# Splitting the low half of each dense weight block into four column pieces on GpSimd

## The chip, the cores and the metric

The kernel runs on one core of a Trainium2 chip. The metric is the time of one execution on the device in microseconds (us); lower is better. Three runs of the kernel before took 2069.74, 2070.41 and 2076.77 us, with a median of 2070.41 us.

The engines are named as in the profile: PE is the matrix engine (PEld its weight loads), DVE is VectorE, ACT is ScalarE, POOL is GpSimd, SP issues most of the transfers.

## The reference

One decoder block over 1024 tokens of width 1024, in float32, with 16 learned tokens put in front. A normalised input goes through two branches side by side, a short gated convolution and a stick-breaking attention with 16 heads of 64; sigmoid gates merge them, an output projection and a gated feed-forward network (width 2816) with a causal depthwise convolution follow.

```python
h = xn @ w_in                                   # (1040, 1024) @ (1024, 8192)
b_c, c_c, h_c, q, k, v, g_conv, g_attn = split(h)
branch_conv = (b_c * causal_dwconv(c_c * h_c, conv_w_mix)) @ w_proj_conv
branch_attn = stick_breaking_attention(q, k, v) @ w_proj_attn
merged = sigmoid(g_conv + b0) * branch_conv + sigmoid(g_attn + b1) * branch_attn
h = h + rms_norm(merged @ w_out)
u, g = split(rms_norm(h) @ w_up_gate)
h = h + rms_norm((gelu(causal_dwconv(u, conv_w_ffn)) * g) @ w_down)
# attention: A[t,s] = sigmoid(z_ts) * prod_{s<j<t} (1 - sigmoid(z_tj)), s < t
```

## The kernel before

**Split operands.** Every product of two float32 matrices is made of three matrix products of a narrower type. An operand x is split into a high half (a copy rounded to the narrower type, written by ACT) and a low half (x minus the high half). The helper `split` at L63 does both: L64 is the copy on ACT, L65 the subtraction on DVE or on the engine it is given. A product is then high·high (L124), high·low (L125) and low·high (L126).

**Dense items.** The class `Dense` (L80) runs a list of 80 items: 64 column blocks of `w_in` (values, queries, keys, the three parts of the convolution, and the two gates), then 8 of `w_proj_conv` and 8 of `w_proj_attn`. One item holds a weight block of 128 rows by 1024 columns: eight blocks of 128 columns, one for each part kb of the contraction. `load` (L96) starts the transfer of the block into a tile `raw`, `prep` (L103) makes the tiles `whi` and `wlo` from it, `run` (L112) prepares item i and i+1, loads i+2, and then issues the products of item i: three chunks of the tokens by eight kb by three products, and after each chunk an evacuation. `raw`, `whi` and `wlo` have two buffers each; a `raw` buffer comes free when the subtraction has read it. Products with the low half read only the 128 columns of `wlo` that belong to their kb.

**The attention beside it.** While the 64 items of `w_in` run, the attention of pair p of heads runs beside the items of pair p+1. `stage1` (L311) makes scores on PE (L326, L327), two sigmoids on ACT (L328 into `fl`, L329 into `be`), a running product over `fl` on DVE (the scan, L336), its product with `be` on POOL (L339), and a mask on POOL (L340). `stage2` (L353) transposes `be` on PE (L373), splits the result into `ah` (ACT) and `al` (DVE, L65), and multiplies it with the values on PE (L363, L364). The convolution of an item runs as `conv3` (L196): one pass on ACT (L197) and two on DVE (L198, L199) over the tile `yy`. The order of emission is a credit scheme written by hand, which spreads items evenly over the pairs; the framework that places instructions and waits can then move an instruction ahead of others on its engine.

**The start and the end of the dense items.** At the start, nine blocks of tokens are normalised (`x_block`, L449: the factor by small DVE operations L72 to L77, the scaling on DVE at L459 for the first three blocks, on POOL at L461 and DVE at L462 for the others) and transposed on PE (L179), with the first two weight blocks prepared between. At the end, each of the last eight items (`item_pa`, L605) multiplies a loaded gate with its result on DVE (L615) and adds on POOL (L616), while the blocks of `w_out` are loaded (L640) and split into the tiles `w_o`, the low half on POOL. These loads share the two `raw` buffers with the dense items, and SP issues them in order.

Of the kernel before, what the change touches and what calls it, by code (L numbers as in the profile page):

```python
# [8 lines left out]
F32 = mybir.dt.float32  # L9
F32R = mybir.dt.float32r  # L10
AF = mybir.ActivationFunctionType
ALU = mybir.AluOpType
# [3 lines left out]
D = 1024  # L16
# [16 lines left out]
def block_kernel(ctx, tc, x, meta_tokens, g_pre_mix, w_in, channels, w_proj_conv,  # L33
                 w_proj_attn, w_out, g_post_mix, g_pre_ffn, w_up_gate, w_down,
                 g_post_ffn, out):
    nc = tc.nc
# [26 lines left out]
    def split(hi, lo, src, lo_engine=None):  # L63
        nc.scalar.copy(hi, src)  # L64
        (lo_engine or nc.vector).tensor_tensor(lo, src, hi.bitcast(F32), op=ALU.subtract)  # L65
# [14 lines left out]
    class Dense:  # L80
# [22 lines left out]
        def prep(self, i):  # L103
            if i < len(self.items) and i not in self.hl:
                self.load(i)
                raw = self.raw.pop(i)
                hi = wpool.tile([P, D], F32R, name="whi", tag="whi")
                lo = wpool.tile([P, D], F32R, name="wlo", tag="wlo")
                split(hi, lo, raw, nc.gpsimd)
                self.hl[i] = (hi, lo)  # L110

        def run(self, i):  # L112
# [915 lines left out]
    for k, _ in enumerate(products(0, *HALF[1], bank_of(ps_o, "po"), evac_u(*HALF[1]))):  # L1028
        if k % 2:
            next(prep, None)  # L1030
# [40 lines left out]
    for i in range(1, len(pairs)):  # L1071
        p, gate = divmod(i, 2)
        if gate:
            conv_gelu(p)
            sets = [products(i, 1, 512, bank, evac_g(p))]
        else:
            sets = [products(i, j0, n, bank, evac_u(j0, n)) for j0, n in HALF]
        for _ in prep:
            pass
        prep = prep_pair(i + 1) if i < last_pair else prep_down_first()  # L1080
        for si, st in enumerate(sets):
            for k, _ in enumerate(st):
                if gate or (7 * si + k) % 2:
                    next(prep, None)
# [45 lines left out]
    for gi, fbs in enumerate(groups):  # L1130
# [14 lines left out]
        for tb in range(8):  # L1145
# [3 lines left out]
            for hf in range(2):  # L1149
                ps = bank()  # L1150
                c = slice(hf * 512, (hf + 1) * 512)
# [6 lines left out]
                a = accs[tb][:, c]  # L1158
# [4 lines left out]
                if last:  # L1163
                    sq = dw.tile([P, 512], F32, name="sq", tag="sq", bufs=2)
                    nc.scalar.activation(sq, a, AF.Square, accum_out=ssqs[tb][:, hf:hf + 1])
                    eng = nc.vector if (tb == 7 and hf) else nc.gpsimd
                    eng.tensor_tensor(a, a, g_post2[:, c], op=ALU.mult)
            next(prep, None)
            if last:
                a, hb, s0 = accs[tb], hbs[tb], ssqs[tb]  # L1170
                nc.vector.tensor_tensor(s0[:, 0:1], s0[:, 0:1], s0[:, 1:2], op=ALU.add)
                r = rstd_of(fsml, s0[:, 0:1], P)
                for hf in range(2):
                    c = slice(hf * 512, (hf + 1) * 512)
# [60 lines left out]
```

## Time and profile before

| | |
|---|---|
| median of 3 runs | 2070.41 us (2069.74 to 2076.77) |
| the profiled execution | 2079.27 us, of it the span from the first to the last instruction 2077.1 us |
| granted PE clock, mean | 0.991 |
| PE busy | 1988.1 us, 12228 matrix instructions |
| DVE busy | 1033.7 us |
| ACT busy | 851.9 us |
| POOL busy | 914.8 us |
| subtractions of the dense blocks on POOL | 80, of 2394 ns each in the mean, 191.5 us in all |

Reading it: "busy" is the time in which an engine has an instruction under way, also one that is held up after it has begun. In a group's row the columns are line, engine, operation, output and inputs, shapes, count; then busy time in us and the mean of one in ns; then the idle time of the engine just before the group's instructions and what ended it. In a row of the timeline the first number is the start in us from the beginning of the span, the second the duration; what stands in square brackets is the idle time before it and what ended that.

The kernel passes through the normalisation of the tokens (to about 60 us), the attention with the dense items of `w_in` (to about 987 us), the last gates and the two branch projections (to about 1262 us), the output projection (to about 1415 us), the up and gate products (to about 1826 us) and the down product.

### The profile page before, as it was taken

To read this page: it belongs to the slowest core of one execution; us is meant where nothing else is said; L and a number is where in the kernel's file an instruction comes from. 1 tells how busy PE (TensorE), PEld (TensorE's weight loads), DVE (VectorE), ACT (ScalarE), POOL (GpSimd) and SP (SyncE) were. 2 spreads that over 40 slices of the span, in tenths; PEclk is the share of its full clock that TensorE was granted. 3 is DMA by queue.
4 is the path that set the end of the run, shared out by engine and by line. 5 is a ranking of instruction groups with operands and counts; after the bars stand their busy time and mean duration, and the time that the engine had idled before them with its cause. 6 is when DMAs were issued, how large, how long until landed. Compare 5 with 4: busy or idle time off the path is not lost.

```text
span 2077.1 us, 30701 instructions
## 1 busy us (share of the span) xinstructions
PE 1988.1 (96%) x12228; PEld 1860.9 (90%) x12228; DVE 1033.7 (50%) x1545; ACT 851.9 (41%) x1771; POOL 914.8 (44%) x764
## 2 busy tenths in 40 slices
PE   5999999999999999999999989979999999999997
PEld 5999999999999999999999989978898899878886
DVE  6445555555555555554232114685444444445546
ACT  4445454545444454545441113354334434412122
POOL 4444444434444444444212551225655656555353
PEclk9999999999999999999999999989999999999999
DMA  3111101111111101111475674313222122253323
GB/s 134 41 51 42 61 31 51 42 41 52 42 51 41 61 32 51 41 48 55 138 231 171 184 189 129 102 54 102 74 90 82 62 102 70 74 182 102 101 81 132
DMA packets 56171, 177.56 MB, mean 85 GB/s; under 512 B 12872, under 2 KB 12872, under 8 KB 56028
## 3 DMA queue, kind: packets, MB, share of 16 engines
q1 hardware_dynamic: 52704, 165.09, 24.5%
q10 hardware_dynamic: 3324, 10.50, 1.6%
q8 instruction: 96, 1.57, 0.3%
q14 instruction: 47, 0.39, 0.1%
HBM read 131.36 MB, written 44.21 MB: 85 GB/s over the span
## 4 chain that ended last, share of the span: by engine, by line
PE 74%; DVE 11%; DMA 6%; ACT 4%; POOL 3%; issue 2%; ACTq 0%; DVEq 0%; POOLq 0%; SPq 0%
PE mm L124 13%; PE mm L125 12%; PE mm L126 12%; PE st L863 6%; PE st L865 5%; PE st L867 5%; PE st L1157 3%; PE st L1155 3%; PE st L1156 3%; PE tp L373 3%; DVE fl L336 3%; PE av L363 2%; PE av L364 2%; DMA xv<-in_x_dram 2%; POOL a_op L65 2%
## 5 line engine op out<-in xcount | busy, mean ns | idle before, releaser
L124 PE MATMUL mm<-xnT,whi 128*128 128x342 f32 (+2 forms) x1536 | 506.8, 330 | 3.6 <-ACT xnT L64 3.6
L125 PE MATMUL mm<-xnT,whi 128*128 128x342 f32 (+2 forms) x1536 | 494.7, 322 | 0.5 <-DVE xnT L65 0.5
L126 PE MATMUL mm<-xnT,wlo 128*128 128x342 f32 (+2 forms) x1536 | 493.0, 321 | 0.0
L339 POOL TENSOR_TENSOR be<-be,fl 114x127 f32<-114x127 f32 (+2 forms) x144 | 178.3, 1238 | 372.3 <-DVE fl L336 350.9
L124 PEld LDWEIGHTS mm<-xnT,whi 128*128 128x128 f32 x1536 | 290.5, 189 | 8.3 <-ACT xnT L64 4.0
L125 PEld LDWEIGHTS mm<-xnT,whi 128*128 128x128 f32 x1536 | 291.1, 190 | 2.1 <-DVE xnT L65 1.0
L126 PEld LDWEIGHTS mm<-xnT,wlo 128*128 128x128 f32 x1536 | 290.5, 189 | 0.0
L336 DVE TENSOR_TENSOR_SCAN fl<-fl,upper 114x128 f32<-114x128 f32 (+2 forms) x144 | 228.0, 1585 | 117.6 <-ACT fl L328 102.8
L65 POOL TENSOR_TENSOR wlo<-raw,whi 128x1024 fp32r<-128x1024 f32 x80 | 191.5, 2394 | 203.5 <-ACT whi L64 203.5
L65 POOL TENSOR_TENSOR a_op<-raw,a_op 128x512 fp32r<-128x512 f32 (+1 forms) x136 | 193.6, 1436 | 88.6 <-ACT a_op L64 86.4
L65 DVE TENSOR_TENSOR al<-tp,ah 128x342 fp32r<-128x342 f32 (+4 forms) x288 | 127.3, 450 | 147.0 <-ACT ah L64 145.7
L64 ACT CAST ah<-tp 128x342 fp32r<-128x342 f32 (+4 forms) x288 | 112.7, 397 | 193.4 <-PE tp L373 185.1
L863 PE MATMUL st<-opT,a_op 128*128 128x258 f32 (+2 forms) x528 | 171.3, 324 | 2.3 <-ACT snap L878 1.1
L865 PE MATMUL st<-opT,a_op 128*128 128x258 f32 (+2 forms) x528 | 169.5, 321 | 2.4 <-DVE opT L65 1.5
L867 PE MATMUL st<-opT,a_op 128*128 128x258 f32 (+2 forms) x528 | 169.3, 321 | 0.0
L328 ACT ACTIVATE fl<-z 114x348 f32<-114x348 f32 (+10 forms) x240 | 111.3, 464 | 127.6 <-PE z L327 123.3
L64 ACT CAST a_op<-raw 128x512 fp32r<-128x512 f32 (+1 forms) x136 | 85.1, 633 | 152.6 <-DVE raw L775 46.0
L373 PE MATMUL tp<-ident,be 114*128 114x114 f32 x720 | 119.5, 263 | 27.7 <-DVE al L65 25.0
L1162 DVE TENSOR_TENSOR acc<-acc,st 128x512 f32<-128x512 f32 x144 | 98.5, 687 | 91.1 <-PE st L1157 91.1
L865 PE MATMUL st<-opB,a_op 128*128 128x512 f32 (+2 forms) x396 | 127.8, 323 | 1.8 <-DVE opB L65 1.8
L863 PE MATMUL st<-opB,a_op 128*128 128x512 f32 (+2 forms) x396 | 127.9, 323 | 0.0
L867 PE MATMUL st<-opB,a_op 128*128 128x512 f32 (+2 forms) x396 | 127.4, 322 | 0.0
(171 smaller groups left out, 4327.6 us busy)
## 6 DMA issues: line engine op xcount, KB each, us to landing
raw<-in_w_in_dram SPq DMA_DIRECT2D x64, 512.0 KB, 3.4
raw<-in_w_up_gate_dram SPq DMA_DIRECT2D x44, 512.0 KB, 3.5
act_d<-owork SPq DMA_DIRECT2D x22, 512.0 KB, 4.2
araw<-act_d SPq DMA_DIRECT2D x22, 512.0 KB
raw<-in_w_down_dram SPq DMA_DIRECT2D x22, 512.0 KB, 3.2
y_d<-yy SPq DMA_DIRECT2D x8, 513.0 KB
ga_d<-gt SPq DMA_DIRECT2D x8, 513.0 KB
o_d<-ot SPq DMA_DIRECT2D x8, 513.0 KB
```

Source lines behind the costliest of these rows:

```text
L64: nc.scalar.copy(hi, src)
L65: (lo_engine or nc.vector).tensor_tensor(lo, src, hi.bitcast(F32), op=ALU.subtract)
L124: nc.tensor.matmul(ps, wh, xh, start=(kb == 0), stop=False)
L125: nc.tensor.matmul(ps, wh, xl, start=False, stop=False)
L126: nc.tensor.matmul(ps, wl, xh, start=False, stop=(kb == KB - 1))
L328: nc.scalar.activation(fl[:, c0:c0 + n], z, AF.Sigmoid, scale=-0.125)
L336: nc.vector.tensor_tensor_scan(fl[:, :nk][:, ::-1], fl[:, :nk][:, ::-1], upper[:, NT - nk:][:, ::-1], 1.0, op0=ALU.mult, op1=ALU.max)
L339: nc.gpsimd.tensor_tensor(be[:, 0:nk - 1], be[:, 0:nk - 1], fl[:, 1:nk], op=ALU.mult)
L373: nc.tensor.transpose(tp[:n, QB * j:QB * (j + 1)], blocks[j][0][:, kb * P:kb * P + n], ident[:QB, :QB])
L863: nc.tensor.matmul(ps, wt[:, 0, k], xh, start=start and kb == 0, stop=False, skip_group_check=True)
L865: nc.tensor.matmul(ps, wt[:, 0, k], xl, start=False, stop=False, skip_group_check=True)
L867: nc.tensor.matmul(ps, wt[:, 1, k], xh, start=False, stop=stop and kb == 3, skip_group_check=True)
```

## The change

`prep` no longer calls the helper. The copy to the high half stays one instruction on ACT over all 1024 columns; the subtraction on POOL is issued in four pieces of 256 columns, in order. What is computed is the same, element for element. Loads, buffers, products and all other calls of the helper stay as they are.

```diff
                 lo = wpool.tile([P, D], F32R, name="wlo", tag="wlo")
-                split(hi, lo, raw, nc.gpsimd)
+                nc.scalar.copy(hi, raw)
+                for a in range(0, D, 256):
+                    c = slice(a, a + 256)
+                    nc.gpsimd.tensor_tensor(lo[:, c], raw[:, c], hi[:, c].bitcast(F32),
+                                            op=ALU.subtract)
                 self.hl[i] = (hi, lo)
```

## The prediction

> **What bounds the kernel now.** First the page's table of engines, then the waits of PE in the attention stretch (60 to 987 us), then the timeline around those waits.
>
> ```profile
> PE 1988.1 (96%) x12228; PEld 1860.9 (90%) x12228; DVE 1033.7 (50%) x1545; ACT 851.9 (41%) x1771; POOL 914.8 (44%) x764
> PE tp L373 <- DVE al L65: 25.0, 22, 2.0
> PE tp L373 <- DVE vv L65: 2.4, 6, 0.4
> PE z L326 <- ACT be L329: 1.2, 1, 1.2
> 60.00:987.00 927.00, 897.90 (x5846) 864.83 (x5845) 500.07 (x686) 462.15 (x1054) 403.73 (x435) 1.00 0.14 47
> ```
>
> PE is the bound, so a change pays only where it closes a hole in PE. The three wait rows are the whole answer for this stretch: 28.6 us of holes, nearly all because a low half `al` or `vv` came late from DVE. No row has PE waiting for `wlo` there, and POOL is busy 403.73 of 927 us. So the weights themselves are early enough; what matters is what their subtraction does to DVE. The timeline of one such hole:
>
> ```profile
> 235.48 2.39 POOL L65 TENSOR_TENSOR wlo<-raw,whi 128x1024 fp32r<-128x1024 f32 x1
> 235.70 4.34 DVE L336 TENSOR_TENSOR_SCAN fl<-fl,upper 114x1040 f32<-114x1040 f32 x1 [1.61 <-ACT fl L328]
> 239.97 0.90 DVE L65 TENSOR_TENSOR al<-tp,ah 128x342 fp32r<-128x342 f32 x2
> 240.51 0.51 PE L373 MATMUL tp<-ident,be 114*128 114x114 f32 x3 [1.48 <-DVE al L65]
> ```
>
> The scan is issued at 235.70, 0.22 us after the subtraction began, and ends at 240.04, which is 2.17 us after the subtraction's end (237.87). It stood still for 2.17 us and then ran for 2.17. Both instructions read two operands from SBUF; `al`, which reads one operand from PSUM, keeps its length. Behind the scan in DVE's queue stands `al`, and PE waits 1.48 us for it. The convolution shows the same:
>
> ```profile
> L198 DVE SCALAR_TENSOR_TENSOR yy<-cc,par,yy 128x1026 f32<-128x1026 f32 x8 | 22.3, 2790 | 12.0 <-ACT yy L197 12.0
> L199 DVE SCALAR_TENSOR_TENSOR yy<-cc,par,yy 128x1026 f32<-128x1026 f32 x8 | 10.2, 1270 | 0.0
> ```
>
> L198 and L199 are the same operation on the same shape; the one that meets the subtraction takes 2790 ns, the other 1270.
>
> The Trainium skill, "SBUF — State Buffer", section "Who interferes with whom", says this: a VectorE instruction with two SBUF inputs and a GpSimd instruction that reads SBUF exclude each other, and whichever starts first keeps the other out for its whole length. The rows agree (2.17 us held, then 2.17 us run).
>
> **The change part by part.** It removes 80 subtractions of 1024 columns and adds 320 of 256; copies, loads and products stay. What does a piece cost?
>
> ```profile
> L65 POOL TENSOR_TENSOR wlo<-raw,whi 128x1024 fp32r<-128x1024 f32 x80 | 191.5, 2394 | 203.5 <-ACT whi L64 203.5
> L339 POOL TENSOR_TENSOR be<-be,fl 114x241 f32<-114x241 f32 x16 | 10.4, 649 | 1.1
> L65 POOL TENSOR_TENSOR w_o<-raw,w_o 128x336 fp32r<-128x336 f32 x1 | 0.9, 856 | 0.0
> ```
>
> No row has 256 columns. The nearest are 241 columns at 649 ns and 336 at 856; on the line between them 256 give 0.68, and I take 0.70 us, nearest to the first. The bounds are 0.60 (a quarter of 2394: no fixed cost at all) and 0.86. A block then costs POOL 2.80 us instead of 2.39, 0.41 more (0 to 1.03). Over 80 blocks that is 33 us on an engine with over half its time free, so by itself it costs nothing; where POOL is on the path it is counted below.
>
> Does a waiting DVE instruction get in between two pieces that follow each other directly? Two places where POOL had two such instructions in a row answer:
>
> ```profile
> 2045.74 2.55 POOL L1167 TENSOR_TENSOR acc<-acc,g_post 128x512 f32<-128x512 f32 x2 [3.40 <-ACT sq L1165]
> 2046.31 0.74 DVE L1171 TENSOR_TENSOR fs<-fs 128x1 f32<-128x1 f32 x1 [0.86 <-ACT sq L1165]
> 1394.15 4.49 POOL L65 TENSOR_TENSOR a_op<-raw,a_op 128x512 fp32r<-128x512 f32 x2 [4.27 <-ACT a_op L64]
> 1395.18 2.31 DVE L65 TENSOR_TENSOR opT<-xr,opT 128x1024 fp32r<-128x1024 f32 x1
> ```
>
> In the first the boundary lies at 2045.74 + 2.55/2 = 2047.02, and `fs`, held since 2046.31, is done at 2047.05, in the middle of the pair. In the second the pair lasts 4.49 us and an `opT` runs within it. So DVE is let in at a boundary, and POOL's next piece then waits for DVE to finish.
>
> Against it stands a rule of the Trainium skill, "GPSIMD Engine Reference", section "2.1 Instruction dispatch": a GpSimd core begins the next instruction when its own share of the last is done, without waiting for the other cores, by which there need be no boundary at all. The two pairs speak against its mattering here; what it would do is the second rival.
>
> Now each kind of hole. The chain of waits has the long scan first at 235.70 and last at 934.64:
>
> ```profile
> 235.70 4.34 DVE fl L336
> 934.64 4.42 DVE fl L336
> ```
>
> That is (934.64 - 235.70) / 6 = 116.5 us apart, seven times, once for each pair of heads but the first.
>
> B, the scan of 1040 columns (rows above): the first piece ends at 235.48 + 0.70 = 236.18, the scan runs to 238.35 instead of 240.04, `al` is 1.69 us earlier than now, and the hole of 1.48 is gone. Late next is POOL: its three other pieces wait out the scan, then take 2.1 us to 240.45 and a memset of 0.95 us behind them; the product L339 for this scan starts at about 241.4, not 240.19. PE has no wait for POOL in this stretch, so I cost these 1.2 us at nothing; without that cover they would take back 1.2 of the 1.48. Seven times 1.48: 10.4 us.
>
> A, the convolution:
>
> ```profile
> 218.18 2.40 POOL L65 TENSOR_TENSOR wlo<-raw,whi 128x1024 fp32r<-128x1024 f32 x1
> 218.79 2.87 DVE L198 SCALAR_TENSOR_TENSOR yy<-cc,par,yy 128x1026 f32<-128x1026 f32 x1 [1.47 <-ACT yy L197]
> 221.58 0.50 DVE L65 TENSOR_TENSOR al<-tp,ah 128x342 fp32r<-128x342 f32 x1
> 222.00 1.27 DVE L199 SCALAR_TENSOR_TENSOR yy<-cc,par,yy 128x1026 f32<-128x1026 f32 x1
> 222.14 0.30 PE L373 MATMUL tp<-ident,be 114*100 114x114 f32 x1 [1.25 <-DVE al L65]
> ```
>
> L198 ran 221.66 - 220.58 = 1.08 us once it was free. The first piece ends at 218.88, just behind its arrival (218.79): then `al` is 1.7 us earlier and the hole of 1.25 closes. If the piece is shorter than 0.61, L198 falls into the second one, is held to 219.4, and some 0.4 us stays. L199 then waits for a piece too (up to 0.70), but it starts from 1 us earlier and has no `al` of a hole right before it. I take 1.05 (0.85 to 1.25), seven times: 7.4 us.
>
> C, two scans one behind the other:
>
> ```profile
> 270.24 2.38 POOL L65 TENSOR_TENSOR wlo<-raw,whi 128x1024 fp32r<-128x1024 f32 x1 [0.30 <-ACT whi L64]
> 271.62 2.23 DVE L336 TENSOR_TENSOR_SCAN fl<-fl,upper 114x584 f32<-114x584 f32 x1
> 274.00 1.21 POOL L339 TENSOR_TENSOR be<-be,fl 114x583 f32<-114x583 f32 x1 [1.38 <-ACT be L329]
> 274.55 2.12 DVE L336 TENSOR_TENSOR_SCAN fl<-fl,upper 114x698 f32<-114x698 f32 x1
> 276.60 0.79 DVE L65 TENSOR_TENSOR al<-tp,ah 128x342 fp32r<-128x342 f32 x2
> 277.14 0.30 PE L373 MATMUL tp<-ident,be 114*100 114x114 f32 x1 [0.51 <-DVE al L65]
> ```
>
> The first scan is held 1.00 us (to 272.62). With boundaries at 270.94, 271.64 and 272.34 it arrives about as the third piece begins, is held 0.72 and leaves one piece over, which moves the product at 274.00 to about 274.2 and keeps the second scan waiting 0.2 longer. The hole before `vv` (0.4) shrinks by 0.3, that before `al` (0.5) grows by as much or more. I count 0; from 0.9 gained, where the second scan gets in ahead of the product, to 0.3 lost, six times. The two `al` waits left of the 22 (7 + 7 + 6 are A, B and C; the longest of all, 2.0 us, is one of the two) I count at 0 as well.
>
> The start:
>
> ```profile
> 13.82 4.67 POOL L65 TENSOR_TENSOR wlo<-raw,whi 128x1024 fp32r<-128x1024 f32 x2 [8.38 <-ACT whi L64]
> 18.45 2.34 POOL L461 TENSOR_TENSOR xn<-xt,gb 128x1024 f32<-128x1024 f32 x1
> 16.42 2.09 DVE L77 TENSOR_TENSOR s<-s,t 128x1 f32<-128x1 f32 x1
> 18.54 3.33 DVE L459 SCALAR_TENSOR_TENSOR xn<-xt,s,gb 128x1024 f32<-128x1024 f32 x1
> 22.02 1.94 PE L179 MATMUL tp<-ident,xn 128*128 128x128 f32 x8 [6.79 <-DVE xn L459]
> ```
>
> `s` is held until the second block's end (18.49), then `xn` until the end of POOL's `xn` (20.79), and PE idles 6.79 us. In pieces, the first block ends at 16.62 and `s` passes there; one piece later, at 17.4, `xn` runs its 1.08 us and ends at 18.5 instead of 21.87, 3.4 us earlier. The three pieces left and POOL's `xn` of the next tokens come 2.2 us later (done at 22.9) and may give part of it back. I take 2.0 (0 to 3.4).
>
> The end of the dense items:
>
> ```profile
> PE mm L124 <- DVE gal L615: 5.2, 1, 5.2
> PE mm L126 <- POOL wlo L65: 2.7, 3, 1.2
> 1220.02 2.37 POOL L65 TENSOR_TENSOR wlo<-raw,whi 128x1024 fp32r<-128x1024 f32 x1
> 1222.41 0.33 SPq L640 DMA_DIRECT2D raw<-in_w_out_dram  x1
> ```
>
> PE waits 2.7 us for `wlo` here, and a first piece lets it begin sooner. But the 5.2 us wait behind it does not come from PE: the load of `w_out` at 1222.41 goes out when the subtraction has released `raw` (1222.39), and the chain goes on through that load. What PE gains it waits longer there, and the last piece, 0.4 us later (0 to 1.0), delays the load and the loads behind it on SP. I take 0.4 lost.
>
> Sum: 10.4 + 7.4 + 0 + 2.0 - 0.4 = 19.4 us less. Against the profiled execution (2079.27 us, of it 2077.1 span) that is 2059.9; it lies 8.9 us over the median, so on the median's scale 2070.4 - 19.4 = 2051.0 us. Bounds: all terms at their best 8.8 + 10.4 + 5.4 + 3.4 = 28.0 less, 2042.4; at their worst 6.0 + 10.4 - 1.8 + 0 - 1.0 = 13.6 less, 2056.8.
>
> **The rivals.**
>
> First, taking turns. Every two-input DVE instruction behind the first waits for a piece of its own, so the four pieces are paid for in full wherever several follow each other. For it: L198 and L199, and the two scans of C. Against: in B only one stands ahead of `al`. Then A keeps its holes, C loses 0.5 six times, the start gives nothing: 10.4 - 3.0 - 0.4 = 7.0 less, 2063.4.
>
> Second, the other side: the pieces hold DVE out as one train. The price is the train's extra length, 0.41 us, at A, B and C (20 times), twice at the start and once at the end: 9.4 us, 2079.8; with pieces of 0.86 it is 23.7 us, 2094. It decides where a held DVE instruction ends: behind the fourth piece instead of the first. It passes the half per cent from pieces of 0.71 on. The pairs at 2045.74 and 1394.15 speak against it.
>
> Third, all holes close, those of C and the two left too: 25.0 + 2.4 + 3.4 = 30.8 less, 2039.6. Against it stands the work that DVE has to do in any case in C.
>
> Fourth, it doesn't do what it says: POOL's other work (products, masks) is placed between the pieces, or the queues come out in another order, so that the meetings fall elsewhere, around 2070.
>
> **How the numbers follow.** About half a per cent, 10.4 us, is what a measurement can tell from no change. Forecast 0.60, turns 0.17, train 0.08, all holes 0.10, another order 0.05. Faster: 0.60 + 0.10 and 0.02 of the turns = 0.72. Same: 0.15 of the turns, 0.03 of the train, 0.03 of the last = 0.21. Slower: 0.05 + 0.02 = 0.07. The range goes from 2041 (below the forecast's best) to 2065 (the turns and a little); the train and most of "all holes" are left out, under 2 in 10.
>
> **What would show it.** Right: L198 at about 1.2 to 1.8 us and the scan of 1040 columns at under 3 where it meets a piece; pieces of 0.65 to 0.75 us, some stretched by a scan to 2 us and more; PE's wait for `al` in the attention down from 25.0 to between 4 and 10 us; the first wait for `xn` at 15 us down by 2 or more. Wrong: a scan of 4.3 us or more beside four pieces (the train), `al` waits moved but not smaller (turns), or PE waiting for a product or mask of POOL, which would say that POOL's lateness had no cover.

## The result, and the profile after

The changed kernel takes 2055.23 us in the median of 4 runs (2054.2 to 2057.31), the kernel before 2073.59 us over the 4 runs taken beside it and earlier (2069.74 to 2078.95). The ratio is 0.9911, with a 95% interval of 0.9883 to 0.9939: 18.4 us or 0.9% faster. The prediction was 19.4 us less than before and a time of 2051.0 us in a range of 2041 to 2065. The time lies 4.2 us above the forecast one; 3.2 of these come from the kernel before, whose median rose from 2070.41 us over three runs to 2073.59 over four.

The page of the kernel after, its engines and the groups that the change touches. Its lines are four further down than in the kernel before: L340 is the scan, L202 and L203 are the convolution, L112 is the pieces.

```profile
PE 1987.5 (97%) x12228; PEld 1861.4 (91%) x12228; DVE 1013.3 (49%) x1545; ACT 851.6 (41%) x1771; POOL 1006.1 (49%) x1004
L112 POOL TENSOR_TENSOR wlo<-raw,whi 128x256 fp32r<-128x256 f32 x320 | 268.7, 871 | 189.9 <-ACT whi L109 189.9
```

PE does the same work in less span, POOL is busy 91 us longer, DVE 20 us shorter. DVE's instructions are the same 1545; what went is time in which they stood still. The pieces' mean of 871 ns holds such standing too, now on POOL's side: the median piece takes 737 ns, the longest 2761.

The waits of PE in the attention, 60 us to 964 us:

```profile
PE tp L377 <- DVE al L65: 7.8, 11, 2.0
PE z L330 <- ACT be L333: 1.3, 1, 1.3
```

The wait for `al` fell from 25.0 us in 22 places to 7.8 in 11, the wait for `vv` is gone, and no wait for POOL has come. The timeline at the long scan, DVE and POOL with the transposes on PE, in the same place of the second pair as the rows of before:

```profile
231.36 4.83 POOL L112 TENSOR_TENSOR wlo<-raw,whi 128x256 fp32r<-128x256 f32 x4
231.58 2.69 DVE L340 TENSOR_TENSOR_SCAN fl<-fl,upper 114x1040 f32<-114x1040 f32 x1 [1.61 <-ACT fl L332]
234.20 0.90 DVE L65 TENSOR_TENSOR al<-tp,ah 128x342 fp32r<-128x342 f32 x2
234.74 0.51 PE L377 MATMUL tp<-ident,be 114*128 114x114 f32 x3
237.04 2.02 POOL L343 TENSOR_TENSOR be<-be,fl 114x1039 f32<-114x1039 f32 x1
```

The scan again arrives 0.22 us after the subtraction began, but takes 2.69 us instead of 4.34: it is let in behind the first piece. The four pieces take 4.83 us, because three of them wait out the scan. At 234.74 PE goes on with its transposes; no idle time stands in that row, where 1.48 us stood before.

The convolution in the second pair, and in the third:

```profile
215.57 4.87 POOL L112 TENSOR_TENSOR wlo<-raw,whi 128x256 fp32r<-128x256 f32 x4
216.19 1.29 DVE L202 SCALAR_TENSOR_TENSOR yy<-cc,par,yy 128x1026 f32<-128x1026 f32 x1 [1.47 <-ACT yy L201]
218.12 0.26 PE L377 MATMUL tp<-ident,be 114*100 114x114 f32 x1
328.37 4.78 POOL L112 TENSOR_TENSOR wlo<-raw,whi 128x256 fp32r<-128x256 f32 x4
329.01 1.88 DVE L202 SCALAR_TENSOR_TENSOR yy<-cc,par,yy 128x1026 f32<-128x1026 f32 x1 [1.47 <-ACT yy L201]
331.37 0.30 PE L377 MATMUL tp<-ident,be 114*100 114x114 f32 x1 [0.27 <-DVE al L65]
```

In the second pair the pass takes 1.29 us and PE goes on without a hole; in the third it takes 1.88, and 0.27 us of the hole stays.

Where the 21.4 us between the two spans (2077.1 and 2055.7) lie. The bounds are the start of PE's first scores, the end of the last product with the values, and the starts of the first output product, the first up product and the first down product. In the kernel before they stand at 76.5, 1015.2, 1254.3, 1363.2 and 1823.0 us; the bounds given further up (987, 1262, 1415 and 1826 us) are rough.

| stretch | before, us | after, us | difference |
|---|---|---|---|
| to the first scores | 76.5 | 73.6 | -2.9 |
| attention | 938.7 | 917.0 | -21.6 |
| last gates, branch projections | 239.1 | 237.7 | -1.4 |
| output projection | 108.9 | 108.0 | -0.9 |
| up and gate products | 459.8 | 464.6 | +4.8 |
| down product and end | 254.1 | 254.7 | +0.6 |

The attention carries all of it. The others are not shown to belong to the change. The up and gate products, which no kernel of this study but the last one touches, lie between 459.8 and 464.6 us in ten profiled executions; the kernel before has the lowest of these times and the kernel after the highest, with a granted clock there of 0.99 and 0.98. The projections take 234.7 us in the fourth kernel below (`e4_b_only`), whose instructions there are those of before, against 239.1.

The prediction's fourth rival, another order, falls by the two traces: the instructions of PE, DVE, ACT and SP come in exactly the same order in both, and those of POOL too but for the pieces. Only in one place, at 19.12 us, does another instruction of POOL stand between two pieces of a block.

### The profile page after: what moved, and what is told of

Same layout as the page of the kernel before. It is cut to its first block, busy times and chain, and to the rows that moved or that the text cites. A ratio compares the mean times of both kernels' runs of the same rounds, so it can differ in the third digit from the quotient of the medians.

```text
span 2055.7 us, 30965 instructions
## 1 busy us (share of the span) xinstructions
PE 1987.5 (97%) x12228; PEld 1861.4 (91%) x12228; DVE 1013.3 (49%) x1545; ACT 851.6 (41%) x1771; POOL 1006.1 (49%) x1004
## 4 chain that ended last, share of the span: by engine, by line
PE 80%; DVE 8%; DMA 4%; ACT 3%; POOL 3%; issue 2%; ACTq 0%; SPq 0%; DVEq 0%; POOLq 0%
PE mm L128 13%; PE mm L129 13%; PE mm L130 13%; PE st L867 6%; PE st L871 6%; PE st L869 6%; PE tp L377 3%; PE st L1161 3%; PE st L1159 3%; PE st L1160 3%; PE av L367 2%; PE av L368 2%; PE z L331 2%; PE z L330 2%; POOL a_op L65 2%
## 5 line engine op out<-in xcount | busy, mean ns | idle before, releaser
L112 POOL TENSOR_TENSOR wlo<-raw,whi 128x256 fp32r<-128x256 f32 x320 | 268.7, 871 | 189.9 <-ACT whi L109 189.9
L340 DVE TENSOR_TENSOR_SCAN fl<-fl,upper 114x128 f32<-114x128 f32 (+2 forms) x144 | 216.5, 1505 | 117.5 <-ACT fl L332 102.9
```

Source lines behind the costliest of these rows:

```text
L112: nc.gpsimd.tensor_tensor(lo[:, c], raw[:, c], hi[:, c].bitcast(F32), op=ALU.subtract)
L340: nc.vector.tensor_tensor_scan(fl[:, :nk][:, ::-1], fl[:, :nk][:, ::-1], upper[:, NT - nk:][:, ::-1], 1.0, op0=ALU.mult, op1=ALU.max)
```

## The experiments

The theory on trial: a subtraction on POOL and a DVE instruction with two SBUF inputs exclude each other for the length of one instruction; a held DVE instruction enters at the next boundary between two POOL instructions; PE's holes in the attention were the time that `al` stood behind a held one.

**Is it the reading, or the long instruction?** The subtraction is replaced by two fills and a subtraction of 8 columns.

```diff
-                split(hi, lo, raw, nc.gpsimd)
+                nc.scalar.copy(hi, raw)
+                for _ in range(2):
+                    nc.gpsimd.memset(lo.bitcast(F32), 0.0)
+                nc.gpsimd.tensor_tensor(lo[:, :8], raw[:, :8], hi[:, :8].bitcast(F32), op=ALU.subtract)
```

> Left out: the low half of the dense weight blocks is set to zero but for its first 8 columns. Each whole subtraction (2.39 us) becomes two fills of all 1024 columns (0.95 us each by the fill of 64 x 1026) and a subtraction of 8 columns; the order on all queues that DVE and PE see stays that of the kernel before. Theory (two instructions that both read SBUF twice exclude each other): fills read nothing, so the long scan takes about 2.2 us wherever it meets them, not 4.34; L198 about 1.3 us, not 2.87; PE's wait for al in the attention falls from 25.0 us to under 6, without any piece of weights being ready earlier than now in a useful way; time 18 to 30 us under before. Rival 1 (any POOL instruction holds DVE up, reading or not): the scan still stands until a fill ends, about 3.1 us, and the wait for al is 8 us or more. Rival 2 (the gain of the pieces comes from PE beginning on the first quarter): no quarter here, so the wait for al stays near 25.

Measured: 2040.42 us (2037.42 to 2042.48), ratio 0.9837 (0.9811 to 0.9862). The timeline of this kernel at the long scan, and its waits of PE:

```profile
230.18 1.97 POOL L111 MEMSET wlo<- 128x1024 f32 x2
230.34 2.32 DVE L339 TENSOR_TENSOR_SCAN fl<-fl,upper 114x1040 f32<-114x1040 f32 x1 [1.61 <-POOL be L343]
PE tp L376 <- DVE al L65: 3.1, 8, 0.8
```

The scan begins 0.16 us into two fills of 0.96 us each in the mean and runs straight through them: 2.32 us. All sixteen scans of this length take 2.32 to 2.33 us. The holes close without any piece. So POOL being busy with fills does no harm, and PE's earlier start on a first quarter is not the cause; the subtraction, which reads, is. Whether one operand read would hold DVE as two do, no run separates. The rule of the Trainium skill ("SBUF — State Buffer", section "Who interferes with whom") that a GpSimd instruction which only writes does not stand in the way of a two-input VectorE instruction agrees with this row. The time went 3 us past the expectation; the projections were 9.5 us shorter in this kernel than before. Of that, 6.1 us are holes of PE (7.8 us before, 1.7 here), where POOL has less to do and some of its work comes in another order. The rest is a shorter busy time of PE, at a granted clock of 1.00 in place of 0.99; why the clock differs is not shown.

**Where the boundary lies.** Two pieces of 512 columns, and eight of 128; the loop of the change with another step.

```diff
-                for a in range(0, D, 256):
-                    c = slice(a, a + 256)
+                for a in range(0, D, 512):
+                    c = slice(a, a + 512)
```

> Two pieces of 512 columns (1.27 us each by the rows of 512). Theory: the long scan is held until the first piece ends, 1.05 us instead of 2.17, so it takes 3.2 us and leaves a hole of 0.4 in PE instead of 1.48; L198 is held 0.65 us, takes 1.75, its hole closes to 0.1; the two scans of the third kind meet the second piece and keep about 1.0. Wait for al in the attention 11 to 15 us, time 12 to 18 us under before. Rival (holds fall with the count of pieces, not with where the boundary lies): half of what four pieces gave, 9 us.

Measured: 2065.1 us (2060.22 to 2068.12), ratio 0.9955 (0.9941 to 0.9969), 8.2 us under before by the medians and 9 by the ratio. That is a miss for the theory as stated (12 to 18) and the number the rival gave, although the wait for `al` came out at 12.9 us, inside the 11 to 15. The rows show why. DVE and POOL of this kernel at the convolution, then PE:

```profile
215.81 3.52 POOL L112 TENSOR_TENSOR wlo<-raw,whi 128x512 fp32r<-128x512 f32 x2
216.44 1.75 DVE L202 SCALAR_TENSOR_TENSOR yy<-cc,par,yy 128x1026 f32<-128x1026 f32 x1 [1.48 <-ACT yy L201]
218.11 0.50 DVE L65 TENSOR_TENSOR al<-tp,ah 128x342 fp32r<-128x342 f32 x1
218.53 1.88 DVE L203 SCALAR_TENSOR_TENSOR yy<-cc,par,yy 128x1026 f32<-128x1026 f32 x1
220.77 0.38 PE L368 MATMUL av<-al,vv 128*128 128x228 f32 x1 [0.55 <-DVE al L65]
```

L202 takes 1.75 us, just as forecast. But the second piece, which waited for it, then holds L203 (1.88 us instead of 1.27), and the `al` behind L203 makes a new hole of 0.55. The holds do follow the boundary; what the expectation left out is the turn that POOL takes in between. The waits of PE show all three kinds (the first row holds, beside the 0.5 us of the third kind, what is left of the long scan's hole, 0.34 to 0.51 us in place of 1.48, forecast 0.4; the last row, the holes before `vv`, rose from 2.4 to 3.3):

```profile
PE tp L377 <- DVE al L65: 8.9, 16, 1.9
PE av L368 <- DVE al L65: 4.0, 7, 0.6
PE tp L377 <- DVE vv L65: 3.3, 6, 0.6
```

> Eight pieces of 128 columns. By the line through 512 columns (1.27) and 1024 (2.39) or the after kernel's 0.70 for 256, a piece takes 0.42 us, a block 3.4. Theory: holes of the first two kinds gone as with four pieces; the first of the two scans of the third kind is held at most 0.42 us instead of 0.74, so PE's hole of 0.84 there shrinks to 0.2 to 0.6; wait for al 4 to 7 us; time 0 to 4 us under that of four pieces. The end of the dense items loses up to 0.6 us a block. Rival (each following instruction of DVE pays for a piece, so the block is paid in full in any case, and it is now a us longer): the holes of the third kind grow to 1 us or more and the time is 3 to 8 us above that of four pieces.

Measured: 2045.59 us (2041.38 to 2054.33), ratio 0.9868 (0.9837 to 0.9899), 9.6 us under four pieces by the medians, more than the 0 to 4 expected. In the profiled executions 7.1 of them lie in the attention (909.9 us against 917.0), where the wait for `al` fell to 2.4 us, under the 4 to 7 expected. Once more on another chip:

> Eight pieces once more, on the chip of the two kernels that build on it, to compare them in the same rounds: 20 to 30 us under before, waits for al in the attention under 4 us.

Measured: 2042.74 us (2039.93 to 2048.33), ratio 0.985 (0.9829 to 0.9872): 31.9 us under the kernel before by the medians, just past the 20 to 30, with 2.4 us of waits for `al`. The waits of PE in the attention of the first of the two runs, and two scans in a row on DVE:

```profile
PE tp L377 <- DVE al L65: 2.4, 3, 1.3
PE z L330 <- ACT be L333: 1.3, 1, 1.3
378.76 1.56 DVE L340 TENSOR_TENSOR_SCAN fl<-fl,upper 114x584 f32<-114x584 f32 x1
380.24 0.85 DVE L65 TENSOR_TENSOR vv<-tp,vv 128x512 fp32r<-128x512 f32 x2
381.02 1.59 DVE L340 TENSOR_TENSOR_SCAN fl<-fl,upper 114x698 f32<-114x698 f32 x1
```

Four pieces left a hole of some 0.84 us here in five of the six pairs. With pieces of 0.46 us (median) the first scan is held 0.2 us (1.56 us, where the shortest of its kind take 1.37) and the second not at all, and the hole is gone, although POOL is busy 350 us with the pieces instead of 269. The rival, that finer pieces cost more than they free, falls.

**Is it additive?** Four pieces in the seven blocks that meet the long scan, the other 73 whole.

```diff
-                for a in range(0, D, 256):
-                    c = slice(a, a + 256)
+                step = 256 if i % 7 == 0 and 14 <= i <= 56 else D
+                for a in range(0, D, step):
+                    c = slice(a, a + step)
```

> Pieces only in the seven blocks whose subtraction meets the scan of 1040 columns; the other 73 blocks are subtracted whole. Theory: exactly the seven holes of 1.48 us close, the others (1.25, and 0.41 with 0.51) stay: wait for al in the attention 25.0 - 10.4 = 14.6 us, first scores of the attention at the same time as before, time 10 us under before (9 to 12). Rival (the gain is general: less time per POOL instruction, earlier quarters in all 80 blocks): 7 of 80 blocks give under 2 us.

Measured: 2065.37 us (2061.21 to 2066.4), ratio 0.9953 (0.9935 to 0.9971), 7.9 us under before. The interval (6.0 to 13.5 us) holds the 10 of the theory and excludes the rival's 2. The waits of PE are sharper than the time:

```profile
PE tp L378 <- DVE al L65: 14.4, 15, 2.0
PE tp L378 <- DVE vv L65: 2.5, 6, 0.4
```

14.4 us in 15 places, where 14.6 was expected and seven places were to go from 22. The long scan takes 2.71 us at 234.24, `yy` keeps its 2784 ns in the mean.

**Length of one instruction or POOL's total?** Each of the four pieces done twice.

```diff
                 for a in range(0, D, 256):
                     c = slice(a, a + 256)
-                    nc.gpsimd.tensor_tensor(lo[:, c], raw[:, c], hi[:, c].bitcast(F32),
-                                            op=ALU.subtract)
+                    for _ in range(2):
+                        nc.gpsimd.tensor_tensor(lo[:, c], raw[:, c], hi[:, c].bitcast(F32),
+                                                op=ALU.subtract)
```

> Each of the four pieces is subtracted twice, so POOL spends some 5.9 us a block in eight instructions of 0.74 us, 2.5 times the one of before. Theory (what counts is how long one instruction keeps DVE out, not how long POOL is busy): the long scan takes 2.5 to 2.8 us as with four pieces, L198 1.3 to 1.9; the waits for al in the attention stay at 6 to 12 us, the time within 5 us of four pieces and 10 us or more under before, although POOL works 190 us more than with four pieces. Rival (POOL's total time beside DVE sets the holds): over 25 us of waits for al and a time above before. If POOL's lateness had no cover, PE would wait for products or masks of POOL.

Measured: 2085.29 us (2082.43 to 2092.37), ratio 1.0051 (1.0029 to 1.0074): slower than before, where the theory had 10 us less, and 30 us above four single pieces, where it had 5. The waits of PE in the attention, the convolution's group, ACT's waits for POOL's product there (this kernel's row, then the row with single pieces), and the waits of PE in the last gates and the projections (1002 to 1257 us):

```profile
PE tp L378 <- DVE al L65: 7.0, 8, 3.0
PE z L331 <- ACT be L334: 7.8, 9, 1.3
L203 DVE SCALAR_TENSOR_TENSOR yy<-cc,par,yy 128x1026 f32<-128x1026 f32 x8 | 11.8, 1469 | 11.8 <-ACT yy L202 11.8
ACT fl L333 <- POOL be L344: 33.6, 11, 4.1
ACT fl L332 <- POOL be L343: 1.7, 2, 1.0
...
PE mm L129 <- DVE gal L620: 6.9, 5, 3.1
PE mm L131 <- POOL wlo L113: 6.0, 8, 2.0
PE mm L129 <- DVE gcl L599: 5.3, 2, 3.1
```

In the attention the theory holds for DVE: `al` waits of 7.0 us against 7.8 with single pieces, L198's counterpart at 1469 ns (1466), the long scan at 2690 ns in the mean (2553). A pair of heads takes 113.9 us, as with single pieces (113.4).

But POOL, busy 252 us longer than with single pieces, is now late, and the sign that the expectation named for this has come by way of ACT. ACT has to wait for POOL's product before it can write `fl` again, 33.6 us in all in place of 1.7. Behind it PE's wait for scores grew from 1.3 to 7.8 us, about 1.0 in five of the seven regular pairs. The first pair takes 6.2 us more. 2.8 of these are one wait for `al` (3.03 us at 133.74, 0.27 with single pieces), which stood behind a scan that came late because ACT had waited 5.36 us for POOL. The projections took 254.2 us, 16.5 more than with single pieces; there PE waits 6.0 us for `wlo` itself (0.9 with single pieces) and 12.2 for `gal` and `gcl`.

So the two costs are apart: how long one instruction lasts sets what DVE loses beside it; how long the block takes in all sets when the weights and POOL's other work are there. The second stayed nearly hidden only in the regular pairs, and the expectation did not ask where it was not.

The length of a pair, from the start of the convolution's first DVE pass in the second and the eighth pair, divided by six, shows the regular pairs alone, without the start and the projections:

| kernel | second pair, us | eighth pair, us | a pair, us |
|---|---|---|---|
| before | 218.79 | 917.74 | 116.5 |
| two pieces | 216.44 | 907.12 | 115.1 |
| pieces for the long scan alone | 217.32 | 906.42 | 114.9 |
| four pieces, each twice | 223.67 | 906.90 | 113.9 |
| four pieces (the change) | 216.19 | 896.85 | 113.4 |
| fills | 214.99 | 889.46 | 112.4 |
| eight pieces | 216.20 | 890.34 | 112.4 |

Eight pieces reach what the fills reach: what is left of the holds (L203 takes 1.47 us in place of 1.27, the long scan 2.43 at 231.82 in place of 2.32) costs PE nothing in the regular pairs.

**What is left.** Two kernels build on eight pieces. In the first, the last eight dense blocks and the blocks of `w_out` take their low half from DVE.

```diff
+                if i < 72:
...
+                else:
+                    nc.vector.tensor_tensor(lo, raw, hi.bitcast(F32), op=ALU.subtract)
...
-                split(w_o[c][:, 0, :, o], w_o[c][:, 1, :, o], rv[:, :, a - i * P:e - i * P], nc.gpsimd)
+                split(w_o[c][:, 0, :, o], w_o[c][:, 1, :, o], rv[:, :, a - i * P:e - i * P], nc.vector)
```

> Eight pieces for the first 72 dense blocks; the last eight blocks and the blocks of w_out take their low half from DVE (1.1 us) in place of POOL (3.4 and 2.2). Theory (PE's wait for gal at the end comes down the chain subtraction, release of raw, load of w_out, its split): the holes of 1.3, 1.2 and 3.1 us there shrink to 1 to 3 us in all, and the time is 2 to 5 us under eight pieces. Rival (the loads themselves set the pace): the holes stay at 4 to 6 us and the time is within 1.5 us of eight pieces.

Measured: 2034.92 us (2031.65 to 2038.49), ratio 0.981 (0.979 to 0.983), 7.8 us under the eight pieces measured beside it. PE has no wait left in the projections, where eight pieces had 4.9 us in three waits for `gal`. The holes closed fully, where 1 to 3 us were expected to stay, and the time passed the 2 to 5 expected. The projections took 7.8 us less (227.7 against 235.5); 5.3 of these are holes, the rest is shorter busy time of PE at a granted clock of 1.00 in place of 0.99, and whether that follows from the edit is not shown. Nor is it shown which of the two moves, the dense blocks or `w_out`, did how much. This is the fastest kernel of the study that computes the whole; it is 39.7 us or 1.9% under before.

In the second, POOL's other long subtractions beside the output projection are cut too.

```diff
-        split(t[:, 0], t[:, 1], raw, nc.gpsimd if b > 5 else nc.vector)
+        if b > 5:
+            nc.scalar.copy(t[:, 0], raw)
+            for k in range(KB):
+                nc.gpsimd.tensor_tensor(t[:, 1, k], raw[:, k], t[:, 0, k].bitcast(F32), op=ALU.subtract)
+        else:
+            split(t[:, 0], t[:, 1], raw)
...
+            for k in range(4):
+                engine.tensor_tensor(t[:, 1, k], q[:, k], t[:, 0, k].bitcast(F32), op=ALU.subtract)
```

> Eight pieces for the dense blocks, and POOL's three subtractions of 912 columns (mb) and two of some 1030 (opB) beside the output projection also in pieces (8 of 114, 4 of some 256). Theory: xv and opB on DVE, held 2.1 and 2.2 us there, are held under 0.8 each; PE's holes in the output projection and the first up products (12.9 us after the start of the 1300s with eight pieces) fall by 1 to 4 us, the one of 6.8 us staying, because DVE's own work stands before it. Rival: those holds lie beside other waits, and nothing changes (within 1 us).

Measured: 2045.52 us (2044.8 to 2047.87), ratio 0.9864 (0.9846 to 0.9883), 2.8 us above eight pieces, with intervals that overlap. No gain shows, so the theory fails and the rival (nothing changes) is the nearer, though its 1 us was passed. Of the nine `xv` one is held in the run of eight pieces measured beside it, 3.40 us long; here it takes 1.69. PE's waits there stay:

```profile
PE tp L754 <- DVE xv L747: 8.2, 2, 6.8
PE st L880 <- DVE opT L65: 2.7, 3, 1.7
```

With eight pieces alone they are 7.6 and 2.0. Before the longest, 6.8 us, DVE works without a break from 1331.6 to 1341.0 us (in eight pieces alone) with none of its instructions held, and then waits 1.5 us for ACT; freeing it of holds elsewhere frees nothing that PE waits for.

## Why the prediction was right

- **The mechanism.** A hold from 0.22 us after the subtraction's begin to its end, with `al` behind it: shown by the fills, which take the hold away and leave POOL busy, and by the seven blocks, which take away seven holes and no others.
- **The handover.** The prediction read from two pairs of POOL instructions that DVE gets in at a boundary. It does: 2.69 us for the scan and 1466 ns in the mean for the convolution's pass, inside the "under 3" and "1.2 to 1.8" that were to show it (two of the eight passes are over, see holes A). The train, the second rival, is out, and with it the bearing here of the rule in the Trainium skill ("GPSIMD Engine Reference", section "2.1 Instruction dispatch") on cores that run on into the next instruction.
- **The piece.** 0.70 us was taken; the median is 0.737, and four in a row unheld take 2.82 (0.705 each).
- **Holes B** (10.4 us; the seven waits add up to 10.5): all closed. POOL's product behind the pieces begins at 237.04, or 5.68 us after the subtraction; before it was 4.71. That is 1.0 us later, where 1.2 were forecast, and no wait of PE came from it, so the cover held. It is not large: with the pieces doubled POOL's lateness reached PE by way of ACT.
- **Holes A** (7.4 us of 8.8): the seven add up to 8.5, since one is 0.99 long, and they closed but for 0.27 us in two pairs, 8.0 us in all. It was close. In five pairs L202 arrives 0.110 to 0.134 us before the recorded end of the first piece and gets in behind it; in the two others it arrives 0.097 to 0.100 us before that end, is held through the second piece too, and takes 1.88 us. The prediction had 0.09 us between the two and gave a shorter piece as the reason for missing the boundary; the pieces there were 0.73 us long. That five of seven were in time is luck; that a late one leaves 0.27 us of the 1.25 is not.
- **Holes C** (0): worked out as a trade and measured as one. The hole before `vv` (0.41) went in all six pairs; the one before `al` grew from 0.5 to 0.84 in five and fell to 0.14 in one, 1.1 us gained in sum. Eight pieces later showed what would have taken the rest away.
- **The attention's sum.** Forecast 17.8 us, measured 21.6. The listed waits for `al` and `vv` fell by 19.6: B 10.5, A 8.0, C 1.2 as the list has it (it leaves out waits of 0.15 us and less), and one of the two counted at nothing halved (0.99 to 0.51), while two small waits are new (0.5 together). The rest is in what counts as busy: PE's busy time there fell by 2.8 us (909.6 to 906.8), nearly all in the dense products of 342 columns. Such a product is drawn 0.32 us long where a hole follows, and the next one starts after 0.16 us where none does, so by these rows a hole cost some 0.16 us more than its wait. The forecast took the waits alone. Waits too short for the list took 0.7 back.
- **The start** (2.0 us): the wait for `xn` at 15 us fell from 6.79 to 3.97, and `xn` ended at 18.57, forecast 18.5. How much of the 2.8 stays is not settled: to the first scores it was 2.9 us less here, but kernels with whole blocks there needed 75.0 and 76.5 us, and four executions with eight pieces 70.8 to 75.0.
- **The end of the dense items** (0.4 us lost): not resolved in the time of the change itself, since executions with the same instructions there differ by 4 us. The trade that it named shows in the waits: for `wlo` 2.7 us before and 0.9 after, for `gal` 5.2 and 6.3. The chain fits what followed: doubling the pieces cost 16.5 us in this stretch, and taking POOL out of it closed every hole.
- **The total.** That 18.4 us came so near to 19.4 is in part luck. In the profiled executions the attention gave 3.8 us more than counted, and the up and gate products, which the sum does not hold, lost 4.8.
- **What the rival "turns" had right.** It is not what happens with four pieces, but it is with two: the second piece holds the second pass, and half the gain at the convolution goes back.

## What to carry to other kernels

A helper engine with time to spare can still cost the bound engine: ask not how long it is busy but how long one of its instructions lasts, what it keeps out for that long, and what stands behind the held instruction in its queue. Cutting such an instruction helps as far as a piece is short against the slack of what waits, and it costs a little more in sum, so cut where another engine is held and not where the cut result itself is awaited. Where the helper stands in series with a load, give the work to an engine that does it in less time.

## What the runs showed of the hardware

- A two-input DVE instruction is let in between POOL instructions queued directly behind each other, in every kernel with pieces; POOL's next piece then waits for it to end (pieces up to 2761 ns long, with 722 at the least). In the rows shown they take turns, one instruction each.
- Who gets in is settled before the recorded end of a piece. With four pieces, the pass of 1026 columns got in where it arrived 0.110 us or more before that end, and was held through the next piece (some 0.61 us longer) where it arrived 0.100 us or less before it; the kernel with doubled pieces has the same split (0.118 and more, 0.102 and less). For the scan of 584 columns the line lies near 0.05 us.
- A small size is no protection from the hold: in the kernel before, an operation on 128 x 1 elements at 16.42 us (0.15 to 0.16 unheld) stood 2.09 us.
- A piece costs 0.46 us at 128 columns, 0.74 at 256 and 1.29 at 512 (medians), with the whole block at 2.40. By these medians I estimate some 0.18 us fixed and 0.28 per 128 columns. Eight pieces take 3.4 us of POOL instead of 2.4, and still win 28 to 32 us of the whole kernel.
